# Two plain blocks in place of three, and two pair sums moved into the preceding stage, in channel mixers 2 to 4

## The chip, the cores and the metric

The kernel runs on one core of a Trainium2 chip. A core has five engines that matter here, each with its own queue of instructions that it works off in order: TensorE (PE; its weight loads are listed apart as PEld), VectorE (DVE), ScalarE (ACT), GpSimd (POOL) and SyncE (SP), which here only issues DMA transfers. The engines meet at semaphores. The metric is the time of one execution on the device, in microseconds (us); lower is better.

## The reference

The reference is a decoder trunk of depth 2 on 512 tokens of width 1024. Each of the two layers is a channel mixer, a token mixer (latent attention in the first layer, sparse attention in the second) and another channel mixer; a last norm ends it. So there are four channel mixers, and the change concerns them alone.

```python
D_MODEL, SEQ, DEPTH, FFN_HIDDEN = 1024, 512, 2, 2816

def rmsnorm(x, g):
    x32 = x.astype(jnp.float32)
    y = x32 * lax.rsqrt(jnp.mean(x32 * x32, axis=-1, keepdims=True) + RMS_EPS)
    return y.astype(x.dtype) * g

def swiglu(x, w_gate, w_up, w_down):
    return (jax.nn.silu(x @ w_gate) * (x @ w_up)) @ w_down

for i in range(DEPTH):
    h = h + 0.5 * swiglu(rmsnorm(h, ffn_norm_a[i]), ffn_a_w_gate[i], ffn_a_w_up[i], ffn_a_w_down[i])
    h = h + mixer_i(rmsnorm(h, mix_norm[i]))
    h = h + 0.5 * swiglu(rmsnorm(h, ffn_norm_b[i]), ffn_b_w_gate[i], ffn_b_w_up[i], ffn_b_w_down[i])
return rmsnorm(h, final_norm)
```

## The kernel before

**Layout.** The residual `h` is kept transposed in eight chunks `h[0]` to `h[7]`, each of 128 channels by 512 tokens. Float32 values go through TensorE as two halves: a rounded high half (a copy on ScalarE) and the remainder as a low half (a subtraction on VectorE). `split` (line 201) makes both. Every product then needs three matmuls: high by high, high by low, low by high. The norm's factor for each token is applied after the gate and up products (`row`, made by `norm_bcast` and a copy), so that products can begin before the norm's sum is known.

**A channel mixer** is `ffn(idx, ...)`, `idx` 0 to 3 for mixers 1 to 4. It works through the hidden width in 22 blocks of 128 rows. The first three (`PLAIN = 3`) are *plain blocks*: `plain` multiplies the gate's weights with all eight chunks, then the up weights, each for both halves of the tokens (L, the first 256, and R), 48 matmuls of 256 columns each.

The other blocks are *summed blocks*. They treat gate and up rows, the two halves of the chunks (0 to 3 and 4 to 7) and the two halves of the tokens as a two by two matrix product, and compute it with seven products in place of eight (the scheme of Strassen and Winograd). For that they need sums and differences on both sides:

- `combine(p)` makes the sums of the pair of chunks p and p+4. Two copies on ScalarE (`y`, line 267) scale the chunks, four differences are taken on VectorE in three instructions (`u`, lines 271 to 273), and one split into a tile `four` ends it. Four pairs serve all summed blocks of a mixer.
- `wsums(idx, f)` makes the sums of block f's weights: it loads the gate's part into `rg` (called `wr` in the profile from the second summed block on) and the up part into `ru`; splits `rg` as it is (`w[1]`, `w[2]`), adds `u0+u1` into `s1` and `g0` into `u0`; splits `ru` (`w[7]`, `w[4]`); adds `s1` into `g0` and `g0` into `g1`; splits `rg` again (`w[6]`, `w[3]`); splits `s1` (`w[5]`).

The seven products of a block (`product`, four pairs by three matmuls each) run in the order 1, 7, 6, 2, 5, 4, 3 on three PSUM banks (`px`, `pq`, `pg`); ScalarE copies parts of them out in between (lines 554 to 561), VectorE adds two parts (lines 562 and 564). The copy in line 561, after product 5, is `evicted`: in the second summed block of a mixer (`f == PLAIN + 1`) the ScalarE half of every split of weights is queued behind the first summed block's `evicted` (`issue_after`, line 365).

After the products come `gate(f)` (lines 437 to 439: a multiplication by `row`, silu on ScalarE, another multiplication), the block's *down units*, and `act(f)` (the product of gate and up, split into `ah` and `al`). A down unit takes three blocks' activations, one output chunk and its slab of the down weights (18 matmuls of 256 columns), and VectorE adds its result to `h` (line 468). Eight units belong to each group of three blocks and are spread as 3, 3 and 2 over the three blocks that follow the group.

**The end of a stage.** The last four blocks' part of the down product (`tail`) runs after all blocks, one output chunk at a time, and each finished chunk goes through `norm_chunk(c)`: it is split for the next stage (`norm_split`) and its squares are summed on ScalarE and POOL. In front of a channel mixer the chunks are finished in the order 0, 4, 1, 5, 2, 6, 3, 7. The token mixers end in the same manner with their output projection (`w_o1`, line 704). So the preceding stages are: for mixer 2 the output projection of the first token mixer, for mixer 3 the down tail of mixer 2, for mixer 4 the output projection of the second token mixer. Mixer 1 has no preceding stage and prepares its chunks itself (`begin`).

**The start of mixers 2 to 4 before.** Plain block 0, the norm's column (`pc`), plain block 1, the row of factors (`pb`), plain block 2, then summed block 3. `combine` is called for pair 0 after block 0, pair 1 after block 1, pairs 2 and 3 after block 2; for mixer 1 pairs 0 and 1, then 2, then 3. The gates and acts of blocks 0 and 1 follow once the row is there. The order of instructions on an engine is made by a scheduler of the framework, which may start an instruction ahead of its place in the program where its operands are ready; `issue_after` binds it.

**Tiles.** The pair sums live in four tiles `four` (2048 columns each) of a pool that the token mixers use as well. Plain slabs and the first split of a summed block share two weight tiles in turn (`wtiles`); the other splits of a summed block and the pair sums' `y` and `u` share three tiles `fh` and three `fl`.

Of the kernel before, what the change touches and what calls it, by code (L numbers as in the profile page):

```python
# [11 lines left out]
F32 = mybir.dt.float32  # L12
# [6 lines left out]
P = 128  # L19
# [4 lines left out]
NF = FF // P  # L24
# [19 lines left out]
TURN = "mm", "S", "T", "mm", "S", "T", "T"  # L44
FGAINS = "a0", "b0", "a1", "b1"
LASTK = 4
HS = S // 2
KP = KC // 2
PLAIN = 3
PAD = 16  # L50
TILES = 24
XC = P + 2
NG = 3
# [8 lines left out]
class Kern:  # L62
# [157 lines left out]
    def norm_chunk(self, c):  # L220
# [5 lines left out]
        else:  # L226
            self.sumsq(self.h[c], self.s2 is None)

    def norm_split(self, c):
        t = self.xp.tile([P, 2 * S], F32R, tag="x", bufs=KC, name="x")  # L230
        if self.to_ffn:

            g = self.ngains[:, self.nng + c : self.nng + c + 1]
            v = t.rearrange("p (e z n) -> p e z n", e=2, z=2)
            hi, lo, src = v[:, :, 0, :], v[:, :, 1, :], self.h[c].rearrange("p (e n) -> p e n", e=2)
            self.split(src, hi, lo, gain=g)
            for e in range(2):
                self.xc["LR"[e], c] = v[:, e, 0, :], v[:, e, 1, :]
        else:
            self.split(self.h[c], t[:, :S], t[:, S:], gain=self.gains[:, self.ng + c : self.ng + c + 1])  # L240
            self.xh.append(t[:, :S])
            self.xl.append(t[:, S:])
# [12 lines left out]
            return self.xp.tile([P, S], F32R, tag="w2", bufs=2, name="q")  # L255
        return self.qt[(self.nq - self.nq // 3 - 1) % 4]

    def combine(self, p):


        nc, fp = self.nc, self.fp
        y = fp.tile([P, 1024], F32, tag="fh", bufs=3, name="y")
        u = fp.tile([P, 1024 + 2 * PAD], F32, tag="fl", bufs=3, name="u")[:, :1024]
        for e in range(2):
            c = p + KP * e
            with self.tc.issue_after(self.weights.ins) if self.weights else nullcontext():
                nc.scalar.activation(y[:, e * S : e * S + S], self.h[c], AF.Copy, scale=self.gains[:, self.ng + c : self.ng + c + 1])
            self.weights = None
        q = lambda t, i: t[:, i * HS : i * HS + HS]
        two = lambda t: t.rearrange("p (a n) -> p a n", n=HS)  # L270
        nc.vector.tensor_tensor(two(u[:, :S]), q(y, 1)[:, None, :].to_broadcast([P, 2, HS]), two(y)[:, 0:4:3, :], op=ALU.subtract)
        nc.vector.tensor_tensor(q(u, 2), q(y, 0), q(u, 1), op=ALU.subtract)
        nc.vector.tensor_tensor(q(u, 3), q(y, 2), q(u, 2), op=ALU.subtract)
        t = self.four()
        self.split(u, t[:, :1024], t[:, 1024:])
        for i, j in enumerate((5, 7, 6, 4)):
            self.xc[j, p] = q(t, i), q(t, i + 4)
        for j, x in zip((1, 2, 3), (("L", p), ("L", p + KP), ("R", p + KP))):
            self.xc[j, p] = self.xc[x]
# [61 lines left out]
    def wsums(self, idx, f):  # L341


        nc, fp, w_gu = self.nc, self.fp, self.a["w_gu"]
        if f == PLAIN:

            rg = fp.tile([P, 1024], F32, tag="fr", bufs=3, name="rg")
        else:
            rg = self.wp.tile([P, 1024], F32, tag="wr", bufs=2, name="wr")
# [6 lines left out]
        def split(src, pool, tag, bufs):  # L356
            n = src.shape[1]
            if pool is self.wp:
                hi, lo = self.wtiles("half")
            elif n == 1024:  # L360
                hi, lo = self.sum_tiles(n)
            else:
                hi = pool.tile([P, n], F32R, tag=tag[0], bufs=bufs, name="wh")
                lo = pool.tile([P, n + 2 * PAD], F32R, tag=tag[1], bufs=bufs, name="wl")[:, 2 * PAD :]
            with self.tc.issue_after(self.evicted.ins) if f == PLAIN + 1 else nullcontext():
                self.split(src, hi, lo)
            return [(hi[:, x : x + S].rearrange("p (k c) -> p k c", c=P), lo[:, x : x + S].rearrange("p (k c) -> p k c", c=P))
                    for x in range(0, n, S)]
# [58 lines left out]
    def ffn(self, idx, gain_next, ap, tp):  # L427
        nc, a = self.nc, self.a
        self.scr, self.fp = (tp, "sq", 1), tp
        ah, al, ht, row = {}, {}, [], None  # L430
        self.pad(ap, 5 * PAD, "pad0")
        tg, tu, units = {}, {}, []

# [9 lines left out]

        def act(f):
            t = tu[f]
            if f < PLAIN:
                t = tu_tile()
                nc.vector.scalar_tensor_tensor(t, tu[f], -1.0, tg[f], op0=ALU.mult, op1=ALU.mult)
            else:
# [45 lines left out]
            return self.norm_col(D, self.s2)  # L495


        gates = [self.bank("T", "pg") for _ in range(PLAIN)]
        for f, g in enumerate(gates):
            u = tu[f] = self.bank(("mm", "S")[f % 2], "pu")  # L500
            if idx == f == 0:
# [29 lines left out]
            elif f:  # L531
                gate(f, g)
                act(f)
            for p in (((0,), (1,), (2, 3)) if idx else ((0, 1), (2,), (3,)))[f]:
                self.combine(p)
        t = self.tiny
        for i, g in enumerate(gates[::-1]):
            nc.scalar.activation(t[:, i + 1 : i + 2], g[:, 0:1], AF.Identity, bias=t[:, i : i + 1])

        tail = PLAIN + (NF - 2 - PLAIN) // NG * NG  # L540
        for f in range(PLAIN, NF):
            if f % NG == 0 and f <= tail:
                units = [partial(unit, b0=f - NG, c=c) for c in range(KC)]
                left = NG if f < tail else NF - tail
            n = -(-len(units) // left)
# [39 lines left out]
        for c in self.order:  # L585
            p = self.mm_bank("pd")
            down(p, self.wslab(a["w_down"][idx, c, :, tail * P :], (NF - tail, P), "act"), tail, NF)
            add(c, p)
            self.norm_chunk(c)
            if ahead and c == self.order[-1]:  # L590
                self.ahead.append(ahead())

# [111 lines left out]
    def w_o1(self, w, oh, ol, c, e, final):  # L704
# [3 lines left out]
        self.nc.vector.tensor_tensor(self.h[c], p, self.h[c], op=ALU.add)  # L708
        if final:
            self.norm_chunk(c)  # L710

    def stats(self, n):

# [820 lines left out]
```

## Time and profile before

| what | us |
|---|---|
| median of 3 runs | 1863.41 |
| lowest and highest | 1863.02, 1865.26 |
| the profiled execution's own time | 1862.05 |
| its span (first to last instruction) | 1860.3 |
| granted TensorE clock | 0.999 of full speed |

How to read the lines below. On the page, the line of the engines gives busy time, its share of the span, and the number of instructions. A line of a group reads: source line, engine, operation, output<-inputs, shapes, count, then busy us and mean ns of one, then the engine's idle time before these instructions and what ended it. A row of the view by windows gives the stretch, its length, then for each engine its busy time and, in parentheses, its instructions that touch the stretch (one that straddles an edge counts in both), then the granted clock, the DMA engines' share and GB/s. A row of the timeline gives start, duration, engine, source line, operation and tiles, and in brackets the engine's idle time before it and what ended that. Matmuls overlap: a matmul of 256 columns is listed with 0.28 us while the next one starts sooner, so PE's pace is read from starts and counts, not from durations. In the same way consecutive VectorE instructions start a little before the listed end of the one before.

In the profiled execution mixer 1 runs from the start to 344 us, mixer 2 from 546 to 881 us, mixer 3 from 881 to 1217 us and mixer 4 from 1513 us; the token mixers lie between.

### The profile page before, as it was taken

Reading aid. Unit: us, or ns where it says so; the run is one execution under the profiler, and the core shown is the slowest. Engines: PE = TensorE matmul, PEld = TensorE weight load, DVE = VectorE, ACT = ScalarE, POOL = GpSimd, SP = SyncE. Lnnn points to the kernel's source line nnn. Section 1 sums busy time; section 2 is a strip of 40 time slices with the busy share of each in tenths; the row PEclk is TensorE's granted clock in tenths of the full one; section 3 lists DMA queues with packets and bytes.
Section 4 is the critical chain, followed back from the end, with each engine's and each line's share of the span. In section 5 each row is a group of like instructions: output and inputs, shape, how many; then the busy total and the mean of one; then the engine's idle time right before and its main releaser. Section 6 shows DMA issues by size and latency. Waiting matters only on the chain.

```text
span 1860.3 us, 37031 instructions
## 1 busy us (share of the span) xinstructions
PE 1845.7 (99%) x14464; PEld 1763.4 (95%) x14464; DVE 1507.4 (81%) x2810; ACT 1064.5 (57%) x1997; POOL 296.7 (16%) x370
## 2 busy tenths in 40 slices
PE   9999999999999999999999999999999999999998
PEld 9999999888889999999999999988888889999997
DVE  8988886688779988886898888666878888888885
ACT  7555553567666555554655545446776865555554
POOL 0000000258830000001000000022666620000000
PEclk9999999999999999999999999999999999999999
DMA  6433331434433433322443332162433133433321
GB/s 238 132 108 103 103 92 48 117 105 103 114 123 112 119 103 109 110 73 72 138 118 110 109 106 81 45 183 82 108 108 103 40 118 116 121 104 107 103 78 69
DMA packets 84351, 196.64 MB, mean 106 GB/s; under 512 B 10944, under 2 KB 38464, under 8 KB 84176
## 3 DMA queue, kind: packets, MB, share of 16 engines
q1 hardware_dynamic: 81664, 191.34, 34.9%
q10 hardware_dynamic: 2512, 2.93, 0.5%
q8 instruction: 114, 1.87, 0.4%
q14 instruction: 61, 0.50, 0.1%
HBM read 178.44 MB, written 2.16 MB: 97 GB/s over the span
## 4 chain that ended last, share of the span: by engine, by line
PE 93%; DVE 3%; ACT 1%; issue 1%; POOL 1%; DMA 0%; ACTq 0%; POOLq 0%; DVEq 0%
PE pd L462 8%; PE pd L464 8%; PE pd L463 8%; PE px L386 6%; PE px L388 6%; PE px L387 5%; PE pg L386 4%; PE pg L388 4%; PE pg L387 4%; PE pq L386 4%; PE pq L388 4%; PE pq L387 4%; PE o L1337 2%; PE pt L1310 2%; PE po L197 2%; PE po L199 2%
## 5 line engine op out<-in xcount | busy, mean ns | idle before, releaser
L462 PE MATMUL pd<-ah,wd 128*128 128x256 f32 x1152 | 318.3, 276 | 0.0
L464 PE MATMUL pd<-ah,wd 128*128 128x256 f32 x1152 | 318.3, 276 | 0.0
L463 PE MATMUL pd<-al,wd 128*128 128x256 f32 x1152 | 318.3, 276 | 0.0
L289 POOL TENSOR_TENSOR s<-s,sq 128x512 f32<-128x512 f32 x38 | 54.7, 1441 | 1050.3 <-ACT sq L285 1050.3
L462 PEld LDWEIGHTS pd<-ah,wd 128*128 128x128 f32 x1152 | 216.3, 188 | 0.0
L464 PEld LDWEIGHTS pd<-ah,wd 128*128 128x128 f32 x1152 | 216.3, 188 | 0.0
L463 PEld LDWEIGHTS pd<-al,wd 128*128 128x128 f32 x1152 | 216.3, 188 | 0.0
L206 DVE TENSOR_TENSOR w<-wr,w 128x1024 fp32r<-128x1024 f32 x72 | 88.2, 1225 | 120.7 <-ACT w L205 120.4
L386 PE MATMUL px<-four,wh 128*128 128x256 f32 x608 | 168.4, 277 | 0.4 <-ACT wh L205 0.2
L388 PE MATMUL px<-four,wl 128*128 128x256 f32 x608 | 168.2, 277 | 0.2 <-DVE wl L206 0.2
L386 PE MATMUL pq<-four,wh 128*128 128x256 f32 x608 | 168.1, 276 | 0.2 <-ACT uq L556 0.2
L387 PE MATMUL px<-four,wh 128*128 128x256 f32 x608 | 168.0, 276 | 0.0
L388 PE MATMUL pq<-four,wl 128*128 128x256 f32 x608 | 167.9, 276 | 0.0
L387 PE MATMUL pq<-four,wh 128*128 128x256 f32 x608 | 167.9, 276 | 0.0
L468 DVE SCALAR_TENSOR_TENSOR h<-pd,h 128x512 f32<-128x512 f32 x216 | 148.3, 686 | 15.4 <-PE pd L464 15.2
L205 ACT ACTIVATE wd<-wdr 128x384 fp32r<-128x384 f32 x192 | 99.2, 519 | 103.8 <-issue 64.6
L176 ACT ACTIVATE w<-wr 128x1024 fp32r<-128x1024 f32 (+3 forms) x89 | 80.8, 908 | 87.5 <-PE pd L464 20.6
L206 DVE TENSOR_TENSOR wd<-wdr,wd 128x384 fp32r<-128x384 f32 x192 | 105.8, 553 | 20.1 <-ACT wd L205 20.0
L178 DVE TENSOR_TENSOR w<-wr,w 128x1024 fp32r<-128x1024 f32 (+3 forms) x75 | 78.3, 1044 | 50.0 <-ACT w L176 49.8
L728 ACT ACTIVATE p<-p,small 128x512 f32<-128x512 f32 (+2 forms) x192 | 106.9, 558 | 19.0 <-DVE small L727 15.3
L386 PEld LDWEIGHTS px<-four,wh 128*128 128x128 f32 x608 | 114.1, 188 | 1.0 <-ACT wh L205 0.4
L388 PEld LDWEIGHTS px<-four,wl 128*128 128x128 f32 x608 | 114.2, 188 | 0.6 <-DVE wl L206 0.6
(379 smaller groups left out, 6264.9 us busy)
## 6 DMA issues: line engine op xcount, KB each, us to landing
wr<-in_w_gu SPq DMA_DIRECT2D x93, 512.0 KB, 3.5
ru<-in_w_gu SPq DMA_DIRECT2D x76, 512.0 KB, 4.3
wdr<-in_w_down SPq DMA_DIRECT2D x192, 192.0 KB, 2.5
wr<-in_w_down SPq DMA_DIRECT2D x24, 256.0 KB, 2.6
wr<-in_mla_w_o SPq DMA_DIRECT2D x8, 512.0 KB, 3.4
th<-btab_d SPq DMA_DIRECT2D x16, 256.0 KB, 3.7
wr<-in_nsa_w_q SPq DMA_DIRECT2D x8, 512.0 KB, 3.8
wr<-in_nsa_w_o SPq DMA_DIRECT2D x8, 512.0 KB, 3.7
```

What stands on the lines that cost most here:

```text
L176: self.copied = nc.scalar.activation(wh[:, m], raw[:, m], AF.Copy)
L178: nc.vector.tensor_tensor(wl[:, m], raw[:, m], f32v(wh[:, m]), op=ALU.subtract)
L205: nc.scalar.activation(hi, src, AF.Copy)
L206: (nc.gpsimd if pool else nc.vector).tensor_tensor(lo, src, f32v(hi), op=ALU.subtract)
L386: mm(out, wh[:, p], xh, start=first and p == 0, stop=False, skip_group_check=True)
L387: mm(out, wh[:, p], xl, start=False, stop=False, skip_group_check=True)
L388: mm(out, wl[:, p], xh, start=False, stop=last and p == KP - 1, skip_group_check=True)
L462: nc.tensor.matmul(o, wh, xh, start=k == b0 and x == 0, stop=False, skip_group_check=True)
L463: nc.tensor.matmul(o, wh, xl, start=False, stop=False, skip_group_check=True)
L464: last = nc.tensor.matmul(o, wl, xh, start=False, stop=k == b1 - 1, skip_group_check=True)
L468: nc.vector.scalar_tensor_tensor(self.h[c], p, 0.5, self.h[c], op0=ALU.mult, op1=ALU.add)
L728: nc.scalar.activation(p_sb[:, :n], p_sb[:, :n], AF.Exp, bias=nm, scale=-1.0, accum_out=sm)
```

## The change

Channel mixers 2 to 4 get two plain blocks, so that block 2 becomes the first summed block; mixer 1 keeps three. The first summed block has no down units beside it; the units begin with block 3 as before, and the down tail still begins at block 18. The order behind `evicted` now holds for block 3 in mixers 2 to 4.

The sums of pairs 0 and 1 are made in the preceding stage: after `norm_chunk(4)` comes `combine(0)`, after `norm_chunk(5)` `combine(1)`. Their `y` and `u` lie in one spare tile of the `four` kind, since the mixer's own tiles don't exist yet. Pairs 2 and 3 are combined after blocks 0 and 1.

```diff
+EARLY = 0, 1
...
-PLAIN = 3
...
+    def combine_early(self, c):
+        if self.to_ffn and c - KP in EARLY:
+            if c == KP:
+                self.spare = self.four(F32)
+            self.combine(c - KP, self.spare)
...
-    def combine(self, p):
+    def combine(self, p, spare=None):
         nc, fp = self.nc, self.fp
-        y = fp.tile([P, 1024], F32, tag="fh", bufs=3, name="y")
-        u = fp.tile([P, 1024 + 2 * PAD], F32, tag="fl", bufs=3, name="u")[:, :1024]
+        if spare is None:
+            y = fp.tile([P, 1024], F32, tag="fh", bufs=3, name="y")
+            u = fp.tile([P, 1024 + 2 * PAD], F32, tag="fl", bufs=3, name="u")[:, :1024]
+        else:
+            y, u = spare[:, :1024], spare[:, 1024:]
...
-        if f == PLAIN:
+        if f == self.plains:
             rg = fp.tile([P, 1024], F32, tag="fr", bufs=3, name="rg")
...
-            with self.tc.issue_after(self.evicted.ins) if f == PLAIN + 1 else nullcontext():
+            with self.tc.issue_after(self.evicted.ins) if f == self.plains + 1 else nullcontext():
                 self.split(src, hi, lo)
...
+        self.plains = 2 if idx else 3
...
-            if f < PLAIN:
+            if f < self.plains:
...
-        gates = [self.bank("T", "pg") for _ in range(PLAIN)]
+        gates = [self.bank("T", "pg") for _ in range(self.plains)]
...
-            for p in (((0,), (1,), (2, 3)) if idx else ((0, 1), (2,), (3,)))[f]:
+            for p in (((2,), (3,)) if idx else ((0, 1), (2,), (3,)))[f]:
                 self.combine(p)
...
-        tail = PLAIN + (NF - 2 - PLAIN) // NG * NG
-        for f in range(PLAIN, NF):
-            if f % NG == 0 and f <= tail:
+        tail, left = (NF - 2) // NG * NG, 1
+        for f in range(self.plains, NF):
+            if f % NG == 0 and NG <= f <= tail:
                 units = [partial(unit, b0=f - NG, c=c) for c in range(KC)]
                 left = NG if f < tail else NF - tail
...
             add(c, p)
             self.norm_chunk(c)
+            self.combine_early(c)
...
         if final:
             self.norm_chunk(c)
+            self.combine_early(c)
```

## The prediction

> **What bounds the kernel now.** I read the page first: the busy shares and the chain that ended last.
>
> ```profile
> span 1860.3 us, 37031 instructions
> ...
> PE 1845.7 (99%) x14464; PEld 1763.4 (95%) x14464; DVE 1507.4 (81%) x2810; ACT 1064.5 (57%) x1997; POOL 296.7 (16%) x370
> ...
> PE 93%; DVE 3%; ACT 1%; issue 1%; POOL 1%; DMA 0%; ACTq 0%; POOLq 0%; DVEq 0%
> ```
>
> PE is on the chain for 93% of the span, so a matmul fewer should shorten it, unless PE then waits for something else. The next view is the one by windows. I cut one long undisturbed stretch, then in mixers 2, 3 and 4 the first two summed blocks (3 and 4), each with its three down units: a window runs from the first product of one block to the first product of the next.
>
> ```profile
> 640.00:840.00 200.00, 200.00 (x1767) 200.00 (x1766) 165.70 (x257) 102.92 (x170) 0.00 (x0) 1.00 0.32 97
> ...
> 580.17:596.13 15.96, 15.96 (x140) 15.76 (x139) 13.10 (x20) 9.59 (x15) 0.00 (x0) 1.00 0.31 91
> 596.13:611.89 15.76, 15.76 (x140) 15.74 (x139) 15.57 (x24) 8.85 (x16) 0.00 (x0) 1.00 0.47 138
> 915.69:931.79 16.10, 15.99 (x141) 15.79 (x139) 12.54 (x19) 9.58 (x15) 0.00 (x0) 1.00 0.22 66
> 931.79:948.06 16.27, 15.93 (x140) 15.74 (x139) 15.56 (x24) 8.77 (x16) 0.00 (x0) 1.00 0.47 134
> 1547.59:1563.79 16.20, 15.96 (x141) 15.77 (x139) 13.34 (x20) 9.60 (x15) 0.00 (x0) 1.00 0.31 91
> 1563.79:1579.92 16.13, 16.13 (x141) 16.01 (x139) 15.84 (x25) 9.02 (x16) 0.00 (x0) 1.00 0.47 136
> ```
>
> The first row gives PE's pace: 200 us hold 1767 matmuls, 0.113 us for each of 256 columns. A plain block issues 96 of them (gate and up, 8 chunks, 2 halves, 3 terms), 10.9 us; a summed block 84 (7 products, 4 pairs, 3 terms), 9.5 us; a down unit 18. Block and three units make 138 matmuls, 15.64 us; the rows' counts are a little higher because matmuls that straddle an edge count twice. So the six windows lose 0.32, 0.12, 0.46, 0.63, 0.56 and 0.49 us, **2.58 us in all**: what mixers 2 to 4 now pay for sums that come late. The long stretch loses nothing: once a mixer runs, VectorE (166 of 200 us) keeps up. The question is only how each mixer starts.
>
> **The change, part by part.**
>
> *Block 2, plain to summed.* Per mixer 96-84=12 matmuls go, 1.36 us; in three mixers **-4.08 us**. All of them lie on PE's path, nothing hides them. The loads stay: two of 512 KB from SP's queue either way. ScalarE and VectorE get other work, whose pace is seen where VectorE's queue runs without a gap:
>
> ```profile
> 553.14 0.68 DVE L271 TENSOR_TENSOR u<-y 128x512 f32<-128x512 f32 x1
> 553.74 0.69 DVE L373 TENSOR_TENSOR ru<-ru,rg 128x512 f32<-128x512 f32 x1
> 554.35 1.22 DVE L206 TENSOR_TENSOR four<-u,four 128x1024 fp32r<-128x1024 f32 x1
> 555.48 1.22 DVE L178 TENSOR_TENSOR w<-wr,w 128x1024 fp32r<-128x1024 f32 x1
> 556.62 0.42 DVE L272 TENSOR_TENSOR u<-y,u 128x256 f32<-128x256 f32 x1
> 556.95 0.69 DVE L271 TENSOR_TENSOR u<-y 128x512 f32<-128x512 f32 x1
> ...
> L267 ACT ACTIVATE y<-h,gains 128x512 f32<-128x512 f32 x32 | 20.8, 708 | 0.0
> ...
> L205 ACT ACTIVATE four<-u 128x1024 fp32r<-128x1024 f32 x16 | 16.8, 1057 | 7.8 <-DVE u L273 7.8
> ```
>
> From start to start VectorE takes 0.60 us for 512 columns, 1.13 for 1024, 0.33 for 256. A plain block costs it two slab splits, gate (2) and act (2): 2x1.13+4x0.60=4.7 us. A summed one costs three wide splits, five narrow operations (two sums over `u`, two over `g`, one split), two evictions of 256, gate and act: 3x1.13+5x0.60+2x0.33+4x0.60=9.5 us. So +4.8 us of VectorE per mixer.
>
> *Two pairs' sums made early.* A pair costs VectorE L271, L272, L273 and one wide split, 0.60+0.33+0.33+1.13=2.4 us, and ScalarE two copies and a split, 2x0.71+1.06=2.5 us at most. They issue no DMA and pass the queues of ScalarE and VectorE only, beside POOL's additions of squares. ScalarE I cost at nothing: in the windows below it is busy for at most 17.6 of 23 us, and where it is late VectorE is later. Two pairs take 4.8 us of VectorE out of the mixer's start: exactly what the summed block puts in. They go here (the end of the stage before and blocks 0 and 1, for mixers 2, 3 and 4; last, the first three summed blocks of mixer 1):
>
> ```profile
> 530.00:545.76 15.76, 15.76 (x71) 13.04 (x70) 12.25 (x16) 10.39 (x16) 7.90 (x5) 1.00 0.33 100
> 545.76:568.80 23.04, 22.99 (x202) 22.81 (x200) 22.06 (x38) 17.59 (x23) 2.85 (x2) 1.00 0.53 185
> 855.33:881.17 25.84, 25.84 (x230) 25.84 (x229) 18.74 (x27) 14.21 (x23) 6.74 (x5) 1.00 0.28 83
> 1497.00:1513.18 16.18, 16.18 (x71) 13.14 (x70) 14.27 (x17) 10.94 (x16) 7.38 (x5) 1.00 0.28 80
> 1513.18:1536.24 23.06, 23.01 (x201) 22.81 (x200) 21.52 (x39) 17.56 (x23) 2.75 (x2) 1.00 0.53 174
> ...
> 40.46:84.38 43.92, 43.41 (x363) 42.03 (x362) 42.38 (x65) 24.12 (x40) 0.00 (x0) 1.00 0.36 113
> ```
>
> VectorE has 7.1 us free in the down tail before mixer 3, but 3.5 and 1.9 us in the two output projections. The sums of block 2 itself should be in time: its weight tile comes free when block 1's gate products end, 48 matmuls or 5.4 us before block 2 starts; the chain that follows (worked out below: 5.8 us without its eviction) has to reach product 6, third in order, whose first low-half matmul is the block's 27th, 2.9 us in. That leaves 2.5 us for VectorE to be busy with other things.
>
> *Block 3 is the new critical place.* Before, block 3 had plain block 2 behind it and block 4 had three units (6.1 us) in front of it. Now block 3 follows block 2 directly, and its splits are still ordered on ScalarE behind the fifth eviction of block 2 (L561, `issue_after`). How long it takes from there to the weights `w[6]` is shown by before's block 4 in mixer 2, which has the same order:
>
> ```profile
> 580.17 0.28 PE L386 MATMUL px<-x,w 128*128 128x256 f32 x1
> ...
> 587.49 0.37 ACT L561 ACTIVATE pg<-px 128x256 f32<-128x256 f32 x1 [0.30 <-PE px L388]
> 587.77 1.05 ACT L205 ACTIVATE w<-wr 128x1024 fp32r<-128x1024 f32 x1
> ...
> 594.61 1.05 ACT L205 ACTIVATE wh<-wr 128x1024 fp32r<-128x1024 f32 x1
> ...
> 588.86 1.23 DVE L206 TENSOR_TENSOR w<-wr,w 128x1024 fp32r<-128x1024 f32 x1
> 590.00 0.42 DVE L564 TENSOR_TENSOR tu<-pq,uq 128x256 f32<-128x256 f32 x1
> 590.34 1.22 DVE L206 TENSOR_TENSOR wl<-ru,wh 128x1024 fp32r<-128x1024 f32 x1
> 591.47 0.69 DVE L437 TENSOR_TENSOR tg<-pg,row 128x512 f32<-128x512 f32 x1
> 592.07 0.69 DVE L375 TENSOR_TENSOR wr<-wr,s 128x512 f32<-128x512 f32 x1
> 592.67 0.69 DVE L468 SCALAR_TENSOR_TENSOR h<-pd,h 128x512 f32<-128x512 f32 x1
> 593.27 0.69 DVE L439 TENSOR_TENSOR tg<-tg,row 128x512 f32<-128x512 f32 x1
> 593.87 0.69 DVE L376 TENSOR_TENSOR wr<-wr 128x512 f32<-128x512 f32 x1
> ...
> 596.27 1.22 DVE L206 TENSOR_TENSOR wl<-wr,wh 128x1024 fp32r<-128x1024 f32 x1
> ```
>
> The eviction comes 7.0 us into a block without its stall of 0.28 us (580.17 to 587.49). Block 3's `w[6]` low half is due 9.5+2.9=12.4 us after block 2 starts: 5.4 us later. The chain took 10.0 us (587.49 to 597.49), with the gate's and the units' VectorE work in between. Its bare steps take 0.28+1.09+1.13+0.60+0.69+1.05+1.22, 6.1 us with the handovers. So PE waits between **0.7 us** and, with before's order but without the two unit additions around it (1.2 us), **3.4 us** in each mixer. PE can fill some of it: products 2 and 4 need none of this chain. The nearest row for such a crowded start is mixer 1's: 252 matmuls of products and 108 of units, 40.8 us of work, in 43.92 us with VectorE busy for 42.38: 1.0 us lost per summed block.
>
> I take 0.8 us for block 3, near the lower end because PE has other products to run, and keep for the two neighbours the 0.86 us (2.58/3) that each mixer loses now: 1.66 us per mixer, **+4.98 us** in place of 2.58. **Sum: -4.08-2.58+4.98=-1.7 us.** The profiled execution took 1862.05 us (span 1860.3 and 1.75 around it), 1.36 under the median of 1863.41; the difference applies to both, and I give the time on the median's scale: **1861.7 us**.
>
> What is hidden: the evictions of block 2 lie under its next products as in any block. The gates and acts of blocks 0 and 1 (8 operations, 4.8 us of VectorE) run beside block 2; in before they ran beside plain block 2, which needed nothing of VectorE but a slab split. That cover is gone, which is why I do not take zero for block 3.
>
> **The rivals.**
>
> *B, the sums come in time.* For it: mixer 2 loses only 0.44 us now, and the start has 4.8 us of pair sums less. With 0.5 us per mixer: -4.08-2.58+1.5=-5.2, **1858.2 us**. Against it: `issue_after` leaves 5.4 us for a chain of at least 6.1.
>
> *C, slower: block 3 waits for the whole chain.* If the gate and act of block 2 go ahead of `wr<-wr,s` on VectorE, as in the rows above, each mixer loses 3.4+0.86=4.3 us: -6.66+12.8=+6.1, **1869.5 us**. It decides from 2.2 us per mixer on, where the sum is zero. Against it: in mixer 1 the order on PE has units between products, and it lost 1.0 us a block.
>
> *D, the early sums hold up the stage before.* Before mixers 2 and 4 VectorE has 3.5 and 1.9 us for 4.8 us of early sums, ahead of which nobody waits, and behind which the splits of the last chunks queue. Before mixer 4 the last of these is already late:
>
> ```profile
> 1518.28 0.38 PE L402 MATMUL pg<-x,w 128*128 128x256 f32 x1
> ...
> 1516.44 1.78 DVE L209 SCALAR_TENSOR_TENSOR x<-h,ngains,x 128x512 fp32r<-128x512 f32 x1
> ...
> 1516.23 1.45 POOL L289 TENSOR_TENSOR s<-s,sq 128x512 f32<-128x512 f32 x1 [0.79 <-ACT sq L285]
> ```
>
> The first gate's matmul waits for that split, and the split took 1.78 us beside an addition on POOL. If what doesn't fit (1.3 and 2.9 us) lands on block 0: -1.7+4.2=+2.5, **1865.9 us**. The Trainium skill speaks for this rival: SBUF — State Buffer, "Who interferes with whom", says that a VectorE instruction with two SBUF inputs and a GpSimd instruction that reads SBUF exclude each other for a whole instruction. All four VectorE operations of a pair have two such inputs; by the rule each could be held by up to one addition. The 1.78 us beside the addition agrees with it.
>
> *E, the early sums aren't early.* The queues don't keep the program's order, so they may still run in blocks 0 and 1. Then the start carries 4.8 us more than before, and mixer 1's loss is the measure, 3.1 us: -6.66+9.3=+2.6, **1866.0 us**.
>
> **How the numbers follow.** My case 0.51, B 0.25, C 0.11, D 0.07, E 0.06. A measurement of this kernel tells about 0.2% (3.7 us) from no change, so faster means below 1859.7 and slower above 1867.1. Faster: most of B and the edge of mine, 0.26. Slower: most of C and the edges of D and E, 0.12. The rest, 0.62, is within. My own case spans 0.7 to 2.6 us per mixer, 1858.9 to 1864.6; the range goes to B's 1858.2 and past D and E, and leaves out C: 1858.0 to 1867.0.
>
> **What would show it.** 14428 matmuls. Windows from block 2's first product: about 9.6 us for block 2, 15.6+0.8 for block 3, 15.8 for block 4. L271 of two pairs before each mixer's first plain matmul (E falls). The first gate of each mixer no longer than before (D falls). In block 3 PE waits at the first `px<-four,wl` for VectorE (mine, C) or not at all (B). The prediction is wrong if PE's pace changes, or if losses appear in the token mixers, which the change should leave alone.

## The result and the profile after

| | before | after |
|---|---|---|
| median of 5 runs, us | 1864.08 | 1881.50 |
| lowest and highest, us | 1863.02, 1865.26 | 1880.60, 1881.93 |
| the profiled execution's own time, us | 1862.05 | 1880.60 |
| granted TensorE clock | 0.999 | 0.996 |

The ratio is 1.0093, 95% interval 1.0081 to 1.0104: the change makes the kernel 17.4 us slower, where 1861.7 was forecast and 1867.0 was the upper end of the range.

The page of the kernel after, the same lines as before; in the chain, the share of each engine:

```profile
span 1878.8 us, 37015 instructions
...
PE 1852.7 (99%) x14428; PEld 1766.8 (94%) x14428; DVE 1529.9 (81%) x2834; ACT 1073.7 (57%) x2012; POOL 300.1 (16%) x370
...
PE 88%; DVE 7%; ACT 2%; issue 1%; DMA 1%; POOL 0%; SPq 0%; DVEq 0%; POOLq 0%; ACTq 0%
```

The 36 matmuls are gone (14428), but VectorE's share of the chain went from 3% to 7%. The view by windows says where. First the down tail before mixer 3 and the first two blocks of mixers 2 and 4; then, for mixers 2, 3 and 4, blocks 2 and 3 with their three units as one stretch, and block 4:

```profile
859.80:892.50 32.70, 29.48 (x230) 28.77 (x229) 24.92 (x35) 18.54 (x29) 9.15 (x5) 0.90 0.22 65
...
548.97:573.41 24.44, 23.67 (x205) 23.27 (x204) 22.72 (x38) 15.36 (x20) 5.19 (x3) 1.00 0.56 195
1526.25:1555.80 29.55, 25.81 (x206) 25.60 (x204) 24.23 (x39) 15.44 (x20) 3.64 (x3) 0.88 0.43 143
...
573.41:600.72 27.31, 26.96 (x225) 26.11 (x224) 26.81 (x41) 17.81 (x33) 0.00 (x0) 1.00 0.35 107
600.72:616.36 15.64, 15.64 (x140) 15.64 (x139) 15.61 (x25) 9.74 (x16) 0.00 (x0) 1.00 0.44 134
915.92:943.47 27.55, 26.86 (x225) 26.20 (x223) 26.53 (x39) 17.14 (x30) 0.00 (x0) 1.00 0.31 104
943.47:959.30 15.83, 15.83 (x142) 15.83 (x141) 15.71 (x26) 9.83 (x16) 0.00 (x0) 1.00 0.33 103
1555.80:1582.89 27.09, 26.86 (x225) 26.13 (x223) 26.19 (x40) 17.73 (x32) 0.00 (x0) 1.00 0.35 107
1582.89:1598.70 15.81, 15.81 (x142) 15.81 (x141) 15.78 (x26) 9.86 (x16) 0.00 (x0) 1.00 0.45 137
```

The tail before mixer 3 takes 32.70 us instead of 25.84 with the same 230 matmuls: +6.86. Mixer 4's first two blocks take 29.55 us where the row of before has 23.06. The row of before ends ahead of the four small matmuls of `pb` and the row of after ends behind them; they take 0.36 us, so the blocks themselves take 6.1 us more. In both stretches the clock column has fallen, to 0.90 and 0.88. Mixer 2's first two blocks take 1.0 us more by the same reckoning.

The starts give the rest. Mixer 2's first matmul is 3.21 us late (545.76, now 548.97). The token mixer ahead of it starts level in both kernels (344.83 and 344.82). When the first early sums run, a matmul of its projection is 1.1 us late already (535.11, now 536.18), for which I have no cause; the other 2.1 us come behind them. The projection before mixer 4 adds 1.6 us: a matmul in it is 11.47 us late (1497.01, now 1508.48), and mixer 4 begins 13.07 us late (1513.18, now 1526.25). The blocks that were to pay for the change, 2 to 4, are not where most of the time went.

The view of PE's waits, kernel after (line waited for, us in total, times, longest), names what it waited for:

```profile
PE pg L412 <- DVE w L178: 3.7, 1, 3.7
PE po L199 <- DVE w L178: 2.9, 2, 1.6
PE pd L474 <- DVE w L178: 1.9, 1, 1.9
...
PE pd L472 <- ACT w L176: 1.3, 1, 1.3
```

None of these four is in the kernel before. All are waits for **weights**: L176 and L178 are the two halves of a slab's split. The worst is mixer 4's first block. The timeline of PE there, then VectorE's and POOL's (start, duration, then the instruction; a count over 1 joins instructions of a kind):

```profile
1526.25 0.28 PE L410 MATMUL pg<-x,w 128*128 128x256 f32 x1
1526.37 0.28 PE L411 MATMUL pg<-x,w 128*128 128x256 f32 x1
1530.39 0.58 PE L412 MATMUL pg<-x,w 128*128 128x256 f32 x1 [3.74 <-DVE w L178]
1530.77 0.41 PE L410 MATMUL pg<-x,w 128*128 128x256 f32 x1
1530.98 0.41 PE L411 MATMUL pg<-x,w 128*128 128x256 f32 x1
```

```profile
1524.76 0.68 DVE L719 TENSOR_TENSOR h<-po,h 128x512 f32<-128x512 f32 x1
1525.36 0.41 DVE L282 TENSOR_TENSOR four<-four 128x256 f32<-128x256 f32 x1
1525.69 2.44 DVE L209 SCALAR_TENSOR_TENSOR x<-h,ngains,x 128x512 fp32r<-128x512 f32 x2
1528.05 2.28 DVE L178 TENSOR_TENSOR w<-wr,w 128x1024 fp32r<-128x1024 f32 x1
1530.26 1.21 DVE L206 TENSOR_TENSOR four<-four 128x1024 fp32r<-128x1024 f32 x1
...
1525.42 1.49 POOL L298 TENSOR_TENSOR s<-s,sq 128x512 f32<-128x512 f32 x1 [0.87 <-ACT sq L294]
1527.80 1.46 POOL L298 TENSOR_TENSOR s<-s,sq 128x512 f32<-128x512 f32 x1 [0.88 <-ACT sq L294]
```

The split of the gate's weights (L178) ends at 1530.3, with an early pair's last subtraction (L282) ahead of it. It takes 2.28 us where it runs beside an addition on POOL. In the kernel before, the same split took 1.21 us and ended 2.1 us ahead of the block's first matmul (1513.18):

```profile
1509.82 1.21 DVE L178 TENSOR_TENSOR w<-wr,w 128x1024 fp32r<-128x1024 f32 x1
```

After the wait PE goes on with 0.21 us from matmul to matmul instead of 0.113. So there are three candidates: the sums' place in VectorE's queue, the stretch beside POOL, and a slow clock behind the wait.

### The profile page after: what moved, and what is told of

It is laid out like the page before. It is cut to its first block, busy times and chain, and to the rows that moved or that the text cites. A ratio compares the mean times of both kernels' runs of the same rounds, so it can differ in the third digit from the quotient of the medians.

```text
span 1878.8 us, 37015 instructions
## 1 busy us (share of the span) xinstructions
PE 1852.7 (99%) x14428; PEld 1766.8 (94%) x14428; DVE 1529.9 (81%) x2834; ACT 1073.7 (57%) x2012; POOL 300.1 (16%) x370
## 3 DMA queue, kind: packets, MB, share of 16 engines
HBM read 178.44 MB, written 2.16 MB: 96 GB/s over the span
## 4 chain that ended last, share of the span: by engine, by line
PE 88%; DVE 7%; ACT 2%; issue 1%; DMA 1%; POOL 0%; SPq 0%; DVEq 0%; POOLq 0%; ACTq 0%
PE pd L474 8%; PE pd L472 8%; PE pd L473 8%; PE px L395 5%; PE px L397 5%; PE px L396 5%; PE pg L395 4%; PE pg L396 4%; PE pg L397 4%; PE pq L395 4%; PE pq L396 4%; PE pq L397 4%; PE o L1349 2%; PE pt L1322 2%; PE pp L199 1%
## 5 line engine op out<-in xcount | busy, mean ns | idle before, releaser
L298 POOL TENSOR_TENSOR s<-s,sq 128x512 f32<-128x512 f32 x38 | 58.3, 1536 | 1062.9 <-ACT sq L294 1062.8
L395 PE MATMUL px<-four,wh 128*128 128x256 f32 x632 | 175.9, 278 | 0.9 <-ACT pg L564 0.6
L397 PE MATMUL px<-four,wl 128*128 128x256 f32 x632 | 174.9, 277 | 0.0
L395 PE MATMUL pq<-four,wh 128*128 128x256 f32 x632 | 174.6, 276 | 0.2 <-ACT uq L566 0.2
L396 PE MATMUL px<-four,wh 128*128 128x256 f32 x632 | 174.6, 276 | 0.0
L397 PE MATMUL pq<-four,wl 128*128 128x256 f32 x632 | 174.6, 276 | 0.0
L396 PE MATMUL pq<-four,wh 128*128 128x256 f32 x632 | 174.5, 276 | 0.0
L395 PEld LDWEIGHTS px<-four,wh 128*128 128x128 f32 x632 | 118.6, 188 | 2.1 <-ACT pg L564 0.9
L176 ACT ACTIVATE w<-wr 128x1024 fp32r<-128x1024 f32 (+3 forms) x83 | 74.3, 896 | 80.0 <-PE pd L474 21.5
L395 PEld LDWEIGHTS pq<-four,wh 128*128 128x128 f32 x632 | 118.6, 188 | 0.4 <-ACT uq L566 0.4
L397 PEld LDWEIGHTS px<-four,wl 128*128 128x128 f32 x632 | 118.6, 188 | 0.1
L396 PEld LDWEIGHTS px<-four,wh 128*128 128x128 f32 x632 | 118.6, 188 | 0.0
```

Source lines behind the costliest of these rows:

```text
L176: self.copied = nc.scalar.activation(wh[:, m], raw[:, m], AF.Copy)
L298: nc.gpsimd.tensor_tensor(self.s2, self.s2, sq, op=ALU.add)
L395: mm(out, wh[:, p], xh, start=first and p == 0, stop=False, skip_group_check=True)
L396: mm(out, wh[:, p], xl, start=False, stop=False, skip_group_check=True)
L397: mm(out, wl[:, p], xh, start=False, stop=last and p == KP - 1, skip_group_check=True)
```

## The experiments

The times are medians; each ratio is taken against runs of the kernel before on the same chip (1863.4 to 1863.9 us in the five groups of runs). In brackets behind a ratio stands its 95% interval.

**The two halves of the change alone.** Two plain blocks with all pairs summed in the mixer, and early sums with three plain blocks:

```diff
-EARLY = 0, 1
+EARLY = ()
...
-            for p in (((2,), (3,)) if idx else ...
+            for p in (((0, 1), (2, 3)) if idx else ...
```

> Two plain blocks in mixers 2 to 4, all four pairs summed in the mixer itself (none in the stage before). Theory: the early sums' instructions, queued ahead of weight splits, cost the 17 us; then the stages before mixers 2 to 4 stand within 0.5 us of the kernel before at each mixer's first matmul, the 36 missing matmuls give 4.1 us back, and the summed blocks lose at most the 4.8 us of DVE work for two pairs in each mixer: 1861 to 1874 us. Rival: the two plain blocks themselves are too short for what has to be ready behind them; then 1876 us or more, with the loss in blocks 2 to 4 of each mixer.

```diff
-        self.plains = 2 if idx else 3
+        self.plains = 3
...
-            for p in (((2,), (3,)) if idx else ...
+            for p in (((2,), (3,), ()) if idx else ...
```

> Three plain blocks, two pairs summed in the stage before, as in the changed kernel. Theory: the delays of 2.5 us before mixer 2, 6.9 us before mixer 3 and 1.7 plus 5.6 us around the start of mixer 4 are all there, and at most 2.6 us of lost time in blocks 3 and 4 goes: 1876 to 1882 us. Rival (the two plain blocks cost the time): 1861 to 1866 us.

Two plain blocks: 1868.3 us, 1.0025 (1.0016 to 1.0034). Early sums: 1880.1 us, 1.0087 (1.0073 to 1.0101). So nearly the whole loss comes with the early sums. The other half doesn't pay either: with all pairs summed in the mixer it loses 4.7 us. The two losses don't simply add up (4.7+16.5 is more than 17.4).

**POOL's additions.** Before mixers 2 to 4 POOL adds up the squares of the chunks (L298). They are left out, first in the kernel after and then, as a control, in the kernel before:

```diff
-            self.sumsq(self.h[c], self.s2 is None)
+            self.sumsq(self.h[c], self.s2 is None, add=not self.to_ffn)
...
-        else:
+        elif add:
             nc.gpsimd.tensor_tensor(self.s2, self.s2, sq, op=ALU.add)
```

> The changed kernel without the additions on POOL of the squared chunks before a mixer (the norm's sum then holds the first chunk and the two late ones only). Theory: the order in the queues carries most of the loss and the stretch of DVE operations beside POOL the smaller part: of the 17 us, the 1.1 us each of five or six stretched operations goes, 1873 to 1878 us. Rival: the exclusion between DVE and POOL carries it; then within 4 us of the kernel before without these additions, 1868 us or less.

> The kernel before without the same additions on POOL (the norm's sum holds the first chunk and the two late ones only): the control for the run above. Theory and rival alike: 1861 to 1864 us, since its PE waits for no DVE operation that stands beside these additions for over 1 us.

1867.8 us, 1.0023 (1.0014 to 1.0032), and the control 1863.8 us, 1.0000 (0.9991 to 1.0008). My theory put the larger part on the queue's order; the rival had it: 13 of the 17 us go with the additions. In the kernel before the same additions cost nothing.

Is it that POOL reads, or that it is busy there at all? Instead of the addition, POOL now writes a constant over the square three times, behind the same waits:

```diff
-            nc.gpsimd.tensor_tensor(self.s2, self.s2, sq, op=ALU.add)
+            for _ in range(3):
+                nc.gpsimd.memset(sq, 0.0)
```

> The changed kernel with each of the additions on POOL before a mixer replaced by three writes of a constant to the squared chunk, at the same place in the queue with the same waits (the norm's sum then holds the first chunk and the two late ones only). First theory (DVE and POOL hold each other up when POOL reads two SBUF tiles): no DVE operation is stretched, 1865 to 1870 us. Rival (it is POOL's place in the order, its waits, or any use of SBUF by POOL): 1876 to 1882 us.

1867.6 us, 1.0023 (1.0015 to 1.0032): the same as without POOL. The timeline of VectorE and POOL at the same place, mixer 4's start, with POOL only writing:

```profile
1515.68 0.69 DVE L722 TENSOR_TENSOR h<-po,h 128x512 f32<-128x512 f32 x1
1516.29 0.41 DVE L282 TENSOR_TENSOR four<-four 128x256 f32<-128x256 f32 x1
1516.62 1.44 DVE L209 SCALAR_TENSOR_TENSOR x<-h,ngains,x 128x512 fp32r<-128x512 f32 x2
1517.98 1.22 DVE L178 TENSOR_TENSOR w<-wr,w 128x1024 fp32r<-128x1024 f32 x1
1519.12 1.22 DVE L206 TENSOR_TENSOR four<-four 128x1024 fp32r<-128x1024 f32 x1
...
1516.72 1.70 POOL L299 MEMSET sq<- 128x512 f32 x3 [1.13 <-ACT sq L294]
```

The order on VectorE is the one of the kernel after, instruction for instruction. But the two L209 take 1.44 us instead of 2.44 and L178 takes 1.22 instead of 2.28, while POOL writes for 1.70 us beside them: 2.06 us gained in five instructions, and there is no wait of 3.7 us. This agrees with the Trainium skill (SBUF — State Buffer, "Who interferes with whom"), which says that a VectorE instruction with two SBUF inputs contends with a GpSimd instruction that reads SBUF, and not with one that only writes it.

**Moving the additions.** Nothing is left out here: all squares but the first go to the mixer's first block, where the last two were made already; and the same with one early pair only:

```diff
-        if self.to_ffn and c in self.order[-2:]:
+        if self.to_ffn and self.s2 is not None:
             self.late.append(c)
```

> The changed kernel with all squares but the first chunk's, and their additions on POOL, made in the mixer's first block, where the last two were made already. First theory: DVE operations stretched by POOL's additions, right ahead of weight splits, carry most of the loss; then the stages before the mixers look as in the run without these additions, and the time is 1865 to 1871 us. Rival: the exclusion only moves into the first two blocks, where it delays the gates, the row or the two late sums: 1873 to 1880 us.

> Two plain blocks, one pair instead of two summed in the stage before, and the squares in the mixer's first block as in the first of these runs. First theory: half of the early DVE work and no additions on POOL beside it leave no wait over 1 us before a mixer; three pairs' sums in two blocks lose at most 1 us more per mixer than two pairs' do: 1862 to 1868 us. Rival: the order in the queues still holds weight splits back: 1870 us or more.

1892.8 us, 1.0159 (1.0146 to 1.0173), and 1891.6 us, 1.0149 (1.0135 to 1.0163): worse than the change itself. The view of PE's waits of the first:

```profile
PE pc L320 <- POOL s L298: 14.7, 3, 7.1
```

Now the norm's column `pc`, which stands in PE's queue, waits for POOL's last addition in each of the three mixers, for up to 7.1 us. Seven additions one behind the other are too long for that place. So these runs say nothing against the stretch, only that this cure is worse than the harm.

**The place in the queue.** Four runs: each early pair's sums bound behind the next output chunk's split; the same with POOL only writing; one early pair with nothing else changed; and one early pair bound behind the split:

```diff
+            with self.tc.issue_after(self.copied.ins), self.tc.issue_after(self.lowed.ins):
                 self.combine(p, self.spare)
```

> The changed kernel with each early pair's sums queued, on ACT and on DVE, behind the split of the next output chunk's weights instead of ahead of it. Theory: most of the loss needs both, sums queued ahead of a split and DVE operations stretched beside POOL; with the order changed a stretch no longer reaches PE at that split, and PE's waits before mixer 3 fall below 1 us and do not halve the clock there: 1866 to 1874 us. Rival (DVE has no room in these stages, whatever the order): 1878 to 1882 us.

> The same order, with POOL's additions before a mixer replaced by writes of a constant (the norm's sum then holds the first chunk and the two late ones only). Theory: the 2.0 us of waits before mixer 3 and 0.8 us at mixer 4 that stayed in the run with the writes alone are the order's: 1863 to 1866 us. Rival (they are DVE's lack of room): within 1 us of that run's 1867.6.

> Two plain blocks, one pair instead of two summed in the stage before, nothing else changed. Theory: half the DVE work leaves fewer operations beside POOL's additions and waits too short to halve the clock; with three pairs' sums in the two blocks, where four cost 4.7 us: 1866 to 1873 us. Rival (any early pair ahead of a split costs as much, since one stretched operation is enough): 1876 us or more.

> One early pair, queued behind the split of the next chunk's weights. Theory: order and amount both help: 1863 to 1868 us, and if the waits before the mixers are all gone, the lowest time of the versions with two plain blocks. Rival (what is left is lost in the mixer's blocks 2 and 3, where DVE has three pairs to sum): 1868 us or more, with no wait over 1 us before a mixer.

1879.3 us, 1.0084 (1.0070 to 1.0098); 1867.9, 1.0025 (1.0014 to 1.0036); 1874.7, 1.0062 (1.0049 to 1.0074); 1874.6, 1.0062 (1.0048 to 1.0076). One pair costs 6.4 us more than none (1868.3), two cost 13.2, and the order seems not to matter. But the traces show that the edges did nothing: VectorE's order before mixers 2, 3 and 4 in the first of these runs is that of the kernel after, because the split named in the edge stood ahead of the sums already. The bound runs measure the same kernels again and don't decide the question. So the sums were bound behind a later split: that of the last output chunk, then that of the mixer's first gate slab.

```diff
+            if c == self.order[-1]:
+                self.flush_early()
...
+            if f == 0 and idx:
+                self.flush_early()
```

(`flush_early` makes the sums held back, behind the last splits issued so far; its first call belongs to the one kernel, the second to the other.)

> The changed kernel with both early pairs' sums queued, on ACT and on DVE, behind the split of the last output chunk's weights. If the place in the queue is what matters, the stage before mixer 3 loses less than 1 us up to the last chunk, but the first gate slab's split now stands behind all of the sums, and mixers 2 and 4 start with a wait of 2 to 4 us: 1870 to 1877 us. If it is DVE's lack of room in the whole stage, the same waits come, only later: 1878 to 1882 us.

> The same, but both pairs' sums queued behind the split of the mixer's first gate slab, so no longer in the stage before. If the place in the queue is what matters: no PE wait over 1 us before a mixer's first block, and about the 1868.3 us of the run with all four pairs summed in the mixer, 1865 to 1870. If sums beside POOL's late additions cost as much as beside the others: 1872 us or more, with the stretch now in block 1.

1872.7 us, 1.0047 (1.0033 to 1.0060), and 1867.9 us, 1.0024 (1.0014 to 1.0034). The profiled execution of the first took 6589 us, so none of its views is used; without it the median of the other five is 1872.0 us. So the place in the queue matters after all: behind the gate's split, the same sums and the same additions on POOL leave none of the four waits. This binding also takes the sums out of the stage before, which is nearly the kernel with all four pairs summed in the mixer (1868.3 us). The first run kept them in that stage, behind its last weights, and brought about 9 of the 13.6 us back. The view of PE's waits of the second kernel, then one early sum on VectorE and the addition on POOL beside it, at mixer 4's start:

```profile
PE px L401 <- ACT pg L572: 1.6, 1, 1.6
...
PE px L403 <- DVE w L206: 1.4, 3, 0.6
...
PE pu L418 <- DVE w L178: 0.8, 1, 0.8
```

```profile
1522.66 1.77 DVE L286 TENSOR_TENSOR four<-four 128x512 f32<-128x512 f32 x1
...
1522.39 1.49 POOL L304 TENSOR_TENSOR s<-s,sq 128x512 f32<-128x512 f32 x1 [1.40 <-ACT sq L300]
```

The early sum is still stretched beside POOL (1.77 us, against 0.68 for this operation in the kernel after at 1514.38). But no weights that PE needs at once stand behind it: the up half's split comes next, and PE waits for that for only 0.8 us. The other waits that stay are in the mixer's own summed blocks (`px`). With both cures at once:

> Early sums behind the first gate slab's split, and POOL's additions before a mixer replaced by writes of a constant (the norm's sum then holds the first chunk and the two late ones only). If the stretch costs time only through the weights behind it, both cures remove the same waits: 1866 to 1869 us, like either alone. If each removes some that the other leaves: 1862 to 1865 us.

1866.1 us, 1.0014 (1.0005 to 1.0023). One cure brings 13 to 14 us, the second 1 to 2 more. So most of the loss takes both: operations stretched beside POOL, and weights in or behind them that PE is waiting for.

**The clock.** The stretches shown explain 2 us of the wait at mixer 4's start, but that start is 6.1 us longer. The view by windows of the kernel after there; the clock is the third column from the end:

```profile
1528.00:1530.00 2.00, 0.00 (x0) 0.00 (x0) 2.00 (x2) 2.00 (x4) 1.25 (x1) 0.73 0.72 244
1530.00:1532.00 2.00, 1.61 (x7) 1.61 (x8) 2.00 (x4) 0.51 (x1) 0.00 (x0) 0.50 0.31 43
1532.00:1534.00 2.00, 2.00 (x12) 2.00 (x11) 2.00 (x4) 1.86 (x3) 0.57 (x1) 0.50 0.94 367
...
1536.00:1538.00 2.00, 2.00 (x20) 2.00 (x20) 1.10 (x3) 1.06 (x1) 0.00 (x0) 1.00 0.78 307
```

Two microseconds touch 12 matmuls at a clock of 0.50 and 20 at 1.00. To tell cause from coincidence, the wait was filled: 20 matmuls that nobody uses, behind the first two of the block.

```diff
+            if self.idle is not None:
+                with self.tc.issue_after(two.ins):
+                    for _ in range(20):
+                        mm(self.idle[:, :HS], wh[:, k], xh, start=True, stop=True, skip_group_check=True)
```

> The changed kernel with 20 more matmuls (20 times 0.113 is 2.3 us) behind the first two of mixer 4's first block, into the bank of the up half that its own first matmul starts anew: they fill part of the 3.7 us in which PE waits there for the split of the weights. If the half clock comes from that wait, the 26 matmuls at 0.213 us behind it fall back to 0.113, and mixer 4 takes 2.3 to 2.6 us less though it holds more matmuls: 1877.5 to 1879.5 us. Rival (the clock falls for another reason): half clock stays, and the time is that of the changed kernel or up to 2.3 us more, 1880.5 to 1883.5 us.

1878.2 us, 1.0078 (1.0065 to 1.0090), 3.3 us less than the kernel after (1.0093; the two intervals overlap a little, so the traces have to bear it out). The timeline of PE, with the 20 as one row, and one row of the view by windows:

```profile
1528.07 0.28 PE L410 MATMUL pg<-x,w 128*128 128x256 f32 x1
1528.18 0.28 PE L411 MATMUL pg<-x,w 128*128 128x256 f32 x1
1528.30 2.52 PE L415 MATMUL pu<-x,w 128*128 128x256 f32 x20
1532.25 0.39 PE L417 MATMUL pg<-x,w 128*128 128x256 f32 x1 [1.43 <-DVE w L178]
1532.47 0.28 PE L410 MATMUL pg<-x,w 128*128 128x256 f32 x1
1532.59 0.28 PE L411 MATMUL pg<-x,w 128*128 128x256 f32 x1
```

```profile
1534.00:1536.00 2.00, 2.00 (x20) 2.00 (x19) 2.00 (x3) 1.82 (x3) 0.71 (x1) 1.00 1.00 377
```

The weights come 4.0 us after the second matmul, as late as before (1528.18 to 1532.25, against 1526.37 to 1530.39), but PE waits for only 1.43 us of it, and the clock stays at 1.00. From mixer 4's first matmul to the end of the span it is 350.4 us instead of 352.6 (1878.5-1528.07, 1878.8-1526.25): twenty useless matmuls save 2.1 us, nearly the 26 times 0.10 us that the half clock cost. In three traces with this wait unfilled (3.7 to 3.8 us: the kernel after, the early sums alone, and the first run that bound them) the clock fell to 0.50 behind it each time. So the half clock at mixer 4's start comes from the wait.

The same in the kernel before, with one weight split made longer in each mixer (`rep` is 3, 4 and 6 for mixers 2, 3 and 4):

```diff
-                if not self.lo_pool:
+                for _ in range(0 if self.lo_pool else rep):
                     nc.vector.tensor_tensor(wl[:, m], raw[:, m], f32v(wh[:, m]), op=ALU.subtract)
```

> The kernel before, with the DVE half of the split of one weight slab written again, 1.22 us each time: the first gate slab of mixer 2 (twice more, 2.4 us), of mixer 3 (three times more, 3.7 us) and of mixer 4 (five times more, 6.1 us). First theory: a wait of PE that reaches about 3.5 us is followed by some 23 matmuls at half clock, 2.3 to 2.6 us on top; then mixer 2 loses at most 2.4 us, mixer 3 up to 6.1 and mixer 4 7.5 to 8.7 us: 1874 to 1881 us. Rival: the clock has nothing to do with the wait, and the delays stay below the DVE work added: 1868 to 1875 us, no half clock.

1880.8 us, 1.0092 (1.0078 to 1.0106). The view of PE's waits, and the windows behind mixer 3's wait:

```profile
PE pc L311 <- POOL s L289: 5.3, 1, 5.3
...
PE pg L403 <- DVE w L178: 3.3, 1, 3.3
```

```profile
888.00:890.00 2.00, 1.12 (x7) 1.12 (x8) 2.00 (x3) 1.06 (x2) 0.35 (x1) 0.85 0.20 16
890.00:892.00 2.00, 2.00 (x11) 2.00 (x11) 2.00 (x3) 0.79 (x2) 2.00 (x1) 0.50 0.69 266
```

Mixer 2, whose longest wait was 1.0 us, kept its clock. Mixer 3 fell to half after the 3.3 us, which two matmuls part from a wait of 1.0 us. So did mixer 4 after 5.3 us (two matmuls behind a wait of 1.5), but there the wait was one I hadn't meant: `pc` waited for POOL's last addition. That addition began late, because the chunk that it squares was finished on VectorE only behind repeated splits; beside VectorE's splits it also took 2.04 us, where such additions took about 1.4.

How long a wait must be, the runs don't tell. Before mixer 3 PE waits once, for 2.48 us, in both runs with one early pair. The view by windows right behind that wait (it ends at 881.46 and at 881.00 us), first with the pair unbound, then bound, which is the same order on VectorE:

```profile
882.00:884.00 2.00, 2.00 (x19) 2.00 (x18) 1.35 (x3) 1.24 (x2) 0.64 (x1) 1.00 0.67 156
...
882.00:884.00 2.00, 2.00 (x13) 2.00 (x13) 0.90 (x2) 0.82 (x2) 1.10 (x1) 0.60 0.73 178
```

In one execution the clock stayed at 1.00, in the other it fell (0.60 on average here, 0.50 from 882.5 us on). With POOL only writing, two waits of 0.95 and 0.77 us before mixer 3 with four matmuls between them were followed by 0.50; with POOL's additions left out, the same two waits were not. So below 3.3 us it isn't the length alone that decides.

**The prediction's own critical place.** It had put the new wait down to block 3's splits, ordered behind block 2's fifth eviction. Without that order, on top of the sums behind the gate's split:

```diff
-            with self.tc.issue_after(self.evicted.ins) if f == self.plains + 1 else nullcontext():
+            with self.tc.issue_after(self.evicted.ins) if f == 4 and not idx else nullcontext():
```

> Early sums behind the first gate slab's split, and block 3's splits in mixers 2 to 4 no longer ordered behind block 2's fifth eviction. If that order is what PE waits for in block 3 (0.7 to 2 us per mixer in the prediction): 1862 to 1866 us. If PE waits there for ScalarE and VectorE as such: within 1 us of 1867.9, or above it where the splits now go ahead of evictions.

1870.1 us, 1.0034 (1.0021 to 1.0047): the median is 2.2 us above the 1867.9 with the order, though the intervals overlap. The view of PE's waits:

```profile
PE px L401 <- ACT pg L572: 4.4, 2, 2.4
```

The splits now go ahead of block 2's evictions on ScalarE, and PE waits for those: 4.4 us at this line, where it was 1.6 with the order. The waits for `w` at `px` (L403, 1.4 us with the order) are gone in return. So the order does hold some weights back, as the prediction had it, but taking it away gains nothing.

## Why the prediction was wrong

**Right: the matmuls.** 36 fewer, at the pace it gave.

**Roughly right: blocks 2 to 4.** At 0.113 us, 222 matmuls are 25.15 us and 138 are 15.64. The three stretches of blocks 2 and 3 lose 2.16, 2.40 and 1.94 us. Block 4 loses nothing: its rows for mixers 3 and 4 run 0.17 and 0.15 us past block 5's first product (959.13 and 1598.55). That makes 6.5 us where the sum had 4.98. With it the sum of those steps is -4.08-2.58+6.5=-0.2 instead of -1.7: a term too small by 1.5 us. The reason given for it, the order behind the eviction, is at most a part of it: without the order the kernel gains nothing.

**Wrong: the moved sums at nothing.** The step "Two pairs' sums made early" took their VectorE work out of the mixer and set nothing against it in the stage before. Only rival D did, with a chance of 0.07, 4.2 us and the wrong measure: how much of 4.8 us fits into the time VectorE has free. In the tail before mixer 3 VectorE had 7.1 us free, and rival D charged it nothing; it lost 6.86 us. The projections, with 3.5 and 1.9 us free, lost 2.1 and 1.6 us, and mixer 4's first blocks 6.1 us more. Free time over a stage says nothing on *when* the operation behind the new one is due. Three things were missing:

1. What stands behind the sums in the queues of ScalarE and VectorE: the weight splits. The text named them ("behind which the splits of the last chunks queue") and priced only the overflow on block 0. ScalarE, which the step costed at nothing, ends one of the four waits (1.3 us). Binding the sums behind the gate's split, and so out of the stage, brought 13.6 us back (1881.5 to 1867.9).
2. The stretch beside POOL. The rule that rival D named and the row that agreed with it, 1.78 us for L209, were in the text, but not in its price. Taking POOL's reading away brought 13.9 us back (1881.5 to 1867.6). Both cures remove nearly the same loss, so these figures are not to be added.
3. The clock. Nothing in the profile of before showed it, as its longest wait of PE is 1.1 us. At mixer 4 it is 26 times 0.10, 2.6 us; in the tail before mixer 3, where the clock column fell to 0.90, the timeline shows 23 matmuls 0.21 us apart, 2.3 us.

The range failed because it went by rival D's price, and that held the smallest part of the mechanism only. With one stretch of 1.0 us, as the row of L209 showed it, in each of the three stages on top of the overflow, that rival would have stood at 1861.7+4.2+3.0=1868.9 us, above the range even without the clock.

**Not settled.** With either cure the kernel stays some 4 us above the one before, and 2.2 us with both. With the sums behind the gate's split, the waits that remain are short and mostly in the summed blocks; no run here took them away. With POOL only writing, waits of 0.95 and 0.77 us and a half clock stay before mixer 3. What decides whether a wait below 3.3 us halves the clock is open, and so is the 1.1 us ahead of the early sums before mixer 2, a loss in a token mixer, which the prediction had named as a sign against itself. None of the versions with two plain blocks beats the kernel before.

## What to carry to other kernels

Work moved "into idle time" of an in-order engine is to be priced at what queues behind it, and by when that is due; the sum of idle time over the stage isn't the measure. Where VectorE operations with two SBUF inputs gain a neighbour on POOL that reads, price each by what a row shows for it beside such a neighbour (here about 1 us more), and ask which weights stand behind it. And a wait of the matmul engine can cost more than its length: here every wait from 3.3 us on did, and some shorter ones.

## What the runs showed of the hardware

- Behind the PE waits of 3.3, 3.7 and 5.3 us shown here the granted clock was 0.50 for 2 us or more. Shorter waits went both ways: a wait of 2.48 us was followed by it in one run and not in another, and two waits of 1.3 and 1.9 us with four matmuls between them, in the tail before mixer 3, were. A gap of 4.0 us of which matmuls filled 2.5 was not. The Trainium skill (TensorE: Matmul & The Clock Gate, "Part 1: The HAM clock gate") gives one idle window of about 3.4 us, free-running, as the condition. A free-running window would let equal waits end differently, as seen here; but waits of 2.48 us and less are shorter than such a window, and there the measurement decides.
- POOL's addition of two 128x512 tiles of 1.46 to 1.49 us lengthened VectorE operations beside it by 1.0 to 1.1 us (1.44 to 2.44 for two, 1.22 to 2.28); three POOL writes at the same place, 1.70 us in all, lengthened none.
- Unused matmuls in a wait kept the clock at 1.00 behind it and made the kernel faster: 1878.2 against 1881.5 us, and 350.4 against 352.6 us from mixer 4's first matmul on.
